# Five small moves in a hybrid decoder trunk: a transfer, two warming matmuls, a maximum, gated products and transposes

## The chip, the cores and the metric

The kernel runs on one core of one Trainium2 chip. The metric is the device time of one execution in microseconds; the median of three runs stands for a kernel. A trace of one more execution shows every instruction of the five engines: TensorE (PE, its weight loads PEld), VectorE (DVE), ScalarE (ACT), GpSimd (POOL) and SyncE (SP, which only issues DMAs).

## The reference

Two layers of a decoder trunk on x of 256 tokens by 2048 features, float32. Cut to what matters here:

```python
# layer 0: h = rms_norm(x); u, v, q, f, i, g = split(h @ w_in)   (1024 columns each)
u = gelu(u); v = rms_norm(gelu(v) per head)
mixed = einsum('hts,bcshd->bcthd', tril(sp_w), v) + sp_b          # gMLP, chunks of 128 tokens
y_a = u * mixed
lb = cumsum(softmax(hgrn_gamma))[0]                               # the "lower bound", 8 heads x 128
# HGRN2, 8 heads: forget gate f' = lb + (1 - lb) * sigmoid(f), k = (1 - lb) * sigmoid(-f),
# o = linear recurrence over q, k, i with decay f'
y_b = rms_norm(o) * silu(g)
x = x + concat(y_a, y_b) @ w_out
x = x + conv_ffn(rms_norm(x))
# layer 1: forgetting attention, 16 heads: scores + c_t - c_s, where
c = cumsum(log_sigmoid(f + b_f))
# softmax, times v, times sigmoid(g), @ w_out; then conv_ffn again
```

## The kernel before

Activations are kept feature-major. Every product with a weight matrix is made at nearly float32 precision from three fast matmuls: an operand is split into a high part and a remainder, and high by high, high by remainder and remainder by high are summed. So each weight chunk (128 x 1024 float32, 512 KB) is loaded by a DMA on SP's queue into `w` (L196), copied by ACT into `wh` (L207), and DVE subtracts the copy from `w` into `wl` (L212). PE then runs twelve matmuls of 512 columns on the chunk (L268 to L270 in `project_tok`, L288 to L290 in `project_four`). `w` has four buffers, `wh` and `wl` three.

The order is written by hand and by a planner. Ahead of each weight chunk the program calls `tick()`, which advances every waiting generator by one step, up to its next `yield`. Side work (norms, heads, gates, transpositions) is written as such generators: one `yield` more puts what follows one weight chunk later. `after(n, g)` starts a generator n + 1 ticks later, and `LAG` (6) ticks are allowed for a transposition to land. A scheduler then gives each engine a fixed order of instructions, by priority and by times of its own; it may take an independent instruction earlier than it is written. `sum_in`, `act_in`, `copy_in`, `mm_in` and `turn_in` tie an instruction behind the latest weight split (`deep["sub"]`), weight copy (`deep["act"]`) or matmul (`deep["main"]`) written so far, so that it can't be taken earlier. At run time every engine works in order: an instruction that waits holds up all that stands behind it.

The start: x comes in seven tiles (1, 1, 2, 2, 2, 4 and 4 of its 16 row blocks). The first is issued on SP, the second on ACT's queue (L87); then the first chunks of the `w_v` projection follow on SP, in halves of 256 KB for the first four (`single` in `weights`), with the other x tiles between them (`AHEAD`, `BEHIND`). `in_order` keeps that order. `WARM` matmuls of 128 columns on a tile of ones (L169) run before the first weights are there; each is two instructions in the trace.

Layer 0 then runs these projections, eight weight chunks each: v (two), f, q, i, f, q, i, u (two), g (two), then the output in four quarters, of which the first two are interwoven. Around the change:

- `mixer_ab` computes lb (L526 to L549) right after v is written. It begins with a maximum over `gam`, which is a part of `pp` that a DMA on ACT's queue brings in late (`fetch_late`); Exp, a reciprocal and products follow, and five small DMAs on POOL's queue spread the result over the partitions (`od`, `orow`).
- `hgrn(h)` is the work of one recurrence head, spread over the ticks of the following projections: products over levels (L601 to L620), scores on PE and their masked copies and additions into `st` on DVE (L625 to L642), then two empty steps, the transpose of `st` on PE (L646, recorded at L165), and one step later the products with i, the mean square (Ln and Exp on ACT, L346, L347) and the scaled copies (L662). `st` and `s128` have three buffers.
- `spatial(j, z)` (L727) waits until all heads are done, takes the gelu of four row blocks of u, and multiplies each into `mg` (L734, recorded at L159), with the split into high part and remainder (L322, L324) as `yB[b]`, one block per step. The output projection reads `yB[0..7]` first. The transposed u (`turn`, tag `QK`, two buffers) stays until its four products are done; the transposed gates of `gated` use the same two buffers.
- `forget()` in `mixer_c` computes c: a scaled copy `ft` on ACT, two transposes on PE (L809, recorded at L165), log-sigmoid, a scan, a store and row broadcasts by POOL's queue, one step apart.
- ACT's functions come in table sets: `act` (L95) loads a set when the function written next needs another (L98), and instructions of one set stay together.

Of the kernel before, what the change touches and what calls it, by code (L numbers as in the profile page):

```python
# [12 lines left out]
ALU = mybir.AluOpType  # L13
# [15 lines left out]
JOIN = 12  # L29
HALF = 8  # L30
EPS = 1e-6
WARM = 7
AHEAD = {2: 2, 4: 4, 6: 6}
BEHIND = {6: 8, 8: 12}
LANE = 64
# [19 lines left out]
def tile_trunk(ctx: ExitStack, tc: tile.TileContext, x, pp_d, cst_d, mlev_d, msk_d,  # L55
               w_v, w_f, w_g, w_i, w_q, w_u, w_abo, w_cf, w_cqkv, w_cg, w_co, w_up, w_dn, spw_d, spb_d, out):
    nc = tc.nc
    V, SC, PE = nc.vector, nc.scalar, nc.tensor
# [20 lines left out]
    fetch = {c0: (t, x[:, c0:c0 + n, :]) for t, c0, n in xload}  # L79
# [4 lines left out]

    first_dma = nc.sync.dma_start(*fetch[0])
    SC.dma_start(pp[:, 0:C_FFN], pp_d[:, 0:C_FFN])
    SC.dma_start(*fetch[1])  # L87
    V.memset(ones, 1.0)
    V.memset(one1, 1.0)
    ident = cst[:, K_ID:K_ID + P]  # L90
# [24 lines left out]
    def bank(tag="px"):  # L115
        n = nm(tag)
        return px.tile([P, 512], F32, tag=tag, name=n, bufs=banks[tag])
# [34 lines left out]
    def act_in(*args, **kw):  # L152
        return behind(act(*args, **kw), "act")
# [4 lines left out]
    def sum_in(*args):  # L158
        return behind(V.tensor_tensor(*args), "sub")  # L159
# [17 lines left out]
    def in_order(r, key="dma"):  # L177
        if key in deep:
            tc.add_manual_dep(r.ins, deep[key].ins.name, order, reason="queue order")
        deep[key] = r  # L180


    def weights(src, n, rows=None, single=None):
        deep["turn"] += 1
        if deep["pool"] is not None and deep["turn"] > 12 and deep["turn"] % 2:
            pool, nw, ns = deep["pool"], 2, 2
        else:
            pool, nw, ns = wp, 4, 3
        w = pool.tile([P, n], F32, tag="w", name=nm("w"), bufs=nw)
        wh = pool.tile([P, n], F32R, tag="wh", name=nm("wh"), bufs=ns)  # L190
        wl = pool.tile([P, n], F32R, tag="wl", name=nm("wl"), bufs=ns)
        parts = [slice(i, i + n // 2) for i in (0, n // 2)] if single else [slice(0, n)]
        for i, p in enumerate(parts):
            if single and i == 0 and single[1] in AHEAD:
                in_order(nc.sync.dma_start(*fetch[AHEAD[single[1]]]))
            r = nc.sync.dma_start(  # L196
                w[:, p] if rows is None else w.rearrange("p (m c) -> p m c", m=rows), src[:, p] if single else src)
            if single:
                in_order(r)
            deep["dma"] = r  # L200
        for i, p in enumerate(parts):
            if single:
                norm, k = single
                r = norm.feed_split(k + i, SC if k + i else V)
                if k + i:
                    in_order(r, "first")
            deep["act"] = SC.activation(wh[:, p], w[:, p], AF.Copy)  # L207
            if single:
                in_order(deep["act"], "first")
            if deep["turn"] == 5:  # L210
                deep["hold"] = deep["act"]
            deep["sub"] = V.tensor_tensor(wl[:, p], w[:, p], wh[:, p].bitcast(F32), ALU.subtract)  # L212
        return wh, wl
# [206 lines left out]
    def mixer_ab(norm):  # L420
# [107 lines left out]
        mx, sm_, lb, omlb = (gm[:, i * NH:(i + 1) * NH] for i in range(4))  # L528
        ge = gm[:, 4 * NH:7 * NH]
        g3 = [gam[:, i * NH:(i + 1) * NH] for i in range(3)]  # L530
        e3 = [ge[:, i * NH:(i + 1) * NH] for i in range(3)]
        V.tensor_tensor(mx, g3[0], g3[1], ALU.max)
        V.tensor_tensor(mx, mx, g3[2], ALU.max)
        for i in range(3):
            V.tensor_tensor(e3[i], g3[i], mx, ALU.subtract)
# [56 lines left out]
        def hgrn(h):  # L592
            l, t = lf[h], kq[h]
            d0 = (h % 4) * P
            SC.activation(l, l, AF.Identity, bias=lb[:, h:h + 1], scale=omlb[:, h:h + 1])
            st = hp.tile([P, 2, P], F32, tag="st", name=nm("st"), bufs=3)
            V.tensor_tensor(st, ident.unsqueeze(1).to_broadcast([P, 2, P]),
                            dgc[:, h].unsqueeze(2).to_broadcast([P, 2, P]), ALU.mult)
            yield

            V.tensor_tensor(t[:, 1::2], t[:, 1::2], view(l, P, (-P, 2), (1, P)), ALU.mult)  # L601
            E = hp.tile([P, NL, 2, P], F32, tag="E", name=nm("E"), bufs=2)
            tot = l
            tots = hp.tile([P, S], F32, tag="tot", name=nm("tot"), bufs=1)
            for li in reversed(range(NL)):
                n = LEVELS[li]
                m = P // n
                for sl in range(2):
                    SC.activation(E[:, li, sl].rearrange("p (b two n) -> p b two n", two=2, n=n),
                                  view(t, 2 * P * sl, (2 * n, 64 // n), (P + n, 2), (1, n)), AF.Copy)  # L610
                if not li:
                    ends = view(t, 0, (P + n, 2), (1, n))
                    V.tensor_tensor(ends, ends, view(tot, 1, (1, 2), (0, n)), ALU.mult)
                    break
                even = view(t, 0, (2 * P, 2), (2 * n, 64 // n), (1, n))
                odd = view(t, P + n, (2 * P, 2), (2 * n, 64 // n), (1, n))
                V.tensor_tensor(even, even, view(tot, 1, (m, 2), (2, m // 2), (0, n)), ALU.mult)
                V.tensor_tensor(odd, odd, view(tot, m, (-m, 2), (2, m // 2), (0, n)), ALU.mult)
                nt = tots[:, S - 2 * m:S - m]
                V.tensor_tensor(nt, view(tot, 0, (2, m)), view(tot, 1, (2, m)), ALU.mult)  # L620
                tot = nt
                if n in (4, 16):
                    yield
            yield
            smk = hp.tile([P, NL * P], F32, tag="smk", name=nm("smk"), bufs=1)  # L625
            for c0, c1 in ((0, 4), (4, NL)):
                sps = bank()
                for li in range(c0, c1):
                    mm_in(sps[:, (li - c0) * P:(li - c0 + 1) * P],
                          E[:, li, 0], E[:, li, 1], start=True, stop=True)  # L630
                if c0 == 0:
                    xps = bank()
                    mm_in(xps[:, 0:P], t[:, 0], t[:, 1], start=True, stop=True)
                    s128 = hp.tile([P, P], F32, tag="s128", name=nm("s128"), bufs=3)
                    SC.activation(s128, xps[:, 0:P], AF.Copy)
                V.tensor_tensor(smk[:, c0 * P:c1 * P], sps[:, 0:(c1 - c0) * P],
                                msk[:, c0 * P:c1 * P], ALU.mult)
                for li in range(c0, c1):
                    n = LEVELS[li]
                    sv = view(st[:, 1], 0, (2 * n, 64 // n), (n - P, 2), (1, n))  # L640
                    V.tensor_tensor(sv, sv, smk[:, li * P:(li + 1) * P].rearrange(
                        "p (b two n) -> p b two n", two=2, n=n), ALU.add)  # L642
            yield
            yield
            op = bank()
            turn_in(op[:, S:S + P], st[:, 1], ident)  # L646
            SC.activation(st[:, 1], op[:, S:S + P], AF.Copy)
            yield
            while len(itoks) <= h // 4:
                yield  # L650
            itok = itoks[h // 4]
            i0, i1 = (itok[:, T, d0:d0 + P] for T in range(2))
            mm_in(op[:, 0:P], st[:, 0], i0, start=True, stop=True)
            PE.matmul(op[:, P:S], s128, i0, start=True, stop=False)
            PE.matmul(op[:, P:S], st[:, 1], i1, start=False, stop=True)
            so = hp.tile([P, LANE], F32, tag="so", name=nm("so"), bufs=2)[:, 0:2]
            for T in range(2):
                SC.activation(itok[:, T, d0:d0 + P], op[:, T * P:(T + 1) * P], AF.Square,
                              accum_out=so[:, T:T + 1])
            rsq(so, so, P)  # L660
            for T in range(2):
                SC.activation(itok[:, T, d0:d0 + P], op[:, T * P:(T + 1) * P], AF.Copy, scale=so[:, T:T + 1])  # L662
            left[0] -= 1
# [63 lines left out]
        def spatial(j, z):  # L727
            while left[0] or j and yB[4 * j - 1] is None:
                yield
            act_in(z, z, AF.Gelu)  # L730
            for i in range(4):
                b = 4 * j + i
                m = mg[b].rearrange("p (t n) -> p t n", t=2)
                sum_in(m, m, natural(z[:, i]), ALU.mult)  # L734
                yB[b] = quad("ya")
                split(yB[b], mg[b], turn=True)
                yield

        for j in range(2):
# [15 lines left out]
    def mixer_c(norm):  # L755
# [44 lines left out]
        def forget():  # L800
# [2 lines left out]
            V.memset(on, 1.0)  # L803
            for T in range(2):
                SC.activation(ft[:, T, 0:CH], pa[T][:, 0:CH], AF.Copy, scale=Rt[:, T:T + 1])
            yield
            ps = bank()
            for T in range(2):
# [405 lines left out]
```

## Time and profile before

| | us |
|---|---|
| median of 3 runs | 2293.24 |
| lowest, highest | 2291.91, 2293.32 |
| the profiled execution | 2294.66 |
| its span, first to last instruction | 2292.5 |
| PE busy | 2284.6 |
| DVE busy | 1561.7 |
| ACT busy | 1314.6 |
| POOL busy | 420.3 |

Matmuls are pipelined: the next one starts 0.23 us after a 512-column matmul, while the trace models an end 0.39 us after the start. So busy time of PE hides short losses, and the distance between two starts shows them. In rows of the timeline the columns are start (us from the span's start), length of the merged group (us), engine, line, operation, tile written and tiles read, count, and in brackets the idle time before and what ended it. "q" behind an engine means its queue, which issues or waits. The list of waits has who waited, for whom, us in total, times and the longest. The profiled execution's granted TensorE clock is given as 1.000; the half speed at the very start shows in the spacing of matmuls alone.

### The profile page before, as it was taken

How to read it: one execution, taken by the hardware profiler on the slowest of the kernel's cores; microseconds unless marked ns; L12 is line 12 of the kernel's file. 1: busy time of each engine (PE TensorE's matmuls, PEld its weight loads, DVE VectorE, ACT ScalarE, POOL GpSimd, SP SyncE). 2: the span in 40 equal slices, each digit the busy share in tenths (PEclk: the TensorE clock that was granted, in tenths of full speed). 3: DMA queues.
4: the chain of work that ended last, by engine and by line, in shares of the span. 5: the costliest groups of instructions: out<-in, count | busy, mean ns of one | idle time of the engine just before them, and what ended most of it. 6: DMA issues, size and time to landing. Idle time of an engine off the chain costs nothing.

```text
span 2292.5 us, 31357 instructions
## 1 busy us (share of the span) xinstructions
PE 2284.6 (100%) x10370; PEld 1899.8 (83%) x10370; DVE 1561.7 (68%) x2374; ACT 1314.6 (57%) x1955; POOL 420.3 (18%) x779
## 2 busy tenths in 40 slices
PE   9999999999999999999999999999999999999999
PEld 7888888888888888888888888888888888888887
DVE  6888767776557656765866665767776467657766
ACT  7677656665456545653555556656665455455643
POOL 0211323212012002111322212232211022012102
PEclk9999999999999999999999999999999999999999
DMA  8655677777667666776676656777777667667765
GB/s 277 213 176 174 188 222 222 239 226 214 202 196 228 212 198 211 221 216 185 176 234 212 198 177 187 214 224 235 232 218 216 195 208 218 211 205 215 220 205 175
DMA packets 487188, 481.05 MB, mean 210 GB/s; under 512 B 102801, under 2 KB 454177, under 8 KB 487025
## 3 DMA queue, kind: packets, MB, share of 16 engines
q1 hardware_dynamic: 459360, 448.29, 63.0%
q0 software_dynamic: 25360, 27.37, 4.9%
q10 hardware_dynamic: 2304, 3.39, 0.4%
q8 instruction: 81, 1.33, 0.2%
q14 instruction: 83, 0.67, 0.1%
HBM read 434.85 MB, written 2.12 MB: 191 GB/s over the span
## 4 chain that ended last, share of the span: by engine, by line
PE 96%; DVE 1%; ACT 1%; DMA 1%; issue 0%; POOL 0%; SPq 0%; DVEq 0%; ACTq 0%
PE pm L290 27%; PE pm L289 27%; PE pm L288 27%; PE pm L269 4%; PE pm L268 4%; PE pm L270 4%; PE px L162 1%; PE pm L259 1%; DVE wl L212 0%; ACT wh L207 0%; DMA w<-in_w_cqkv 0%; DMA pp<-in_pp 0%; PE px L165 0%; PE pm L233 0%; ACT L98 0%
## 5 line engine op out<-in xcount | busy, mean ns | idle before, releaser
L212 DVE TENSOR_TENSOR wl<-w,wh 128x1024 fp32r<-128x1024 f32 (+1 forms) x812 | 986.2, 1217 | 634.1 <-ACT wh L207 630.4
L207 ACT ACTIVATE wh<-w 128x1024 fp32r<-128x1024 f32 (+1 forms) x812 | 854.4, 1054 | 770.9 <-PE pm L290 580.0
L288 PE MATMUL pm<-wh,a 128*128 128x512 f32 x1792 | 700.0, 391 | 0.0
L289 PE MATMUL pm<-wl,a 128*128 128x512 f32 x1792 | 697.6, 389 | 1.0 <-DVE wl L212 1.0
L290 PE MATMUL pm<-wh,a 128*128 128x512 f32 x1792 | 697.5, 389 | 0.0
L314 POOL DMA_DIRECT2D zt<-tmp x413 | 223.6, 549 | 1199.4 <-DVE tmp L308 983.1
L289 PEld LDWEIGHTS pm<-wl,a 128*128 128x128 f32 x1792 | 336.6, 188 | 70.9 <-DVE wl L212 1.8
L290 PEld LDWEIGHTS pm<-wh,a 128*128 128x128 f32 x1792 | 336.4, 188 | 70.2
L288 PEld LDWEIGHTS pm<-wh,a 128*128 128x128 f32 x1792 | 336.5, 188 | 69.2
L314 POOL DMA_DIRECT2D turn<-tmp x336 | 182.0, 550 | 557.0 <-DVE tmp L308 315.7
L288 PE MATMUL pm<-wh,hid 128*128 128x512 f32 x688 | 267.6, 389 | 0.0
L289 PE MATMUL pm<-wl,hid 128*128 128x512 f32 x688 | 267.6, 389 | 0.0
L290 PE MATMUL pm<-wh,hid 128*128 128x512 f32 x688 | 267.6, 389 | 0.0
L268 PE MATMUL pm<-wh,a 128*128 128x512 f32 x464 | 183.7, 397 | 0.0
L269 PE MATMUL pm<-wl,a 128*128 128x512 f32 x464 | 181.1, 390 | 0.9 <-DVE wl L212 0.9
L270 PE MATMUL pm<-wh,a 128*128 128x512 f32 x464 | 180.9, 390 | 0.0
L289 PEld LDWEIGHTS pm<-wl,hid 128*128 128x128 f32 x688 | 129.1, 188 | 27.0
L288 PEld LDWEIGHTS pm<-wh,hid 128*128 128x128 f32 x688 | 129.1, 188 | 26.8
L290 PEld LDWEIGHTS pm<-wh,hid 128*128 128x128 f32 x688 | 129.1, 188 | 26.7
L308 DVE STREAM_TRANSPOSE tmp<-z 128x512 f32<-128x512 f32 x132 | 92.3, 706 | 21.1 <-ACT z L993 18.4
L156 ACT ACTIVATE conv<-zt,pp 128x256 f32<-128x256 f32 x176 | 95.3, 588 | 16.0 <-DMA zt<-tmp 11.0
L269 PEld LDWEIGHTS pm<-wl,a 128*128 128x128 f32 x464 | 87.2, 188 | 19.6 <-DVE wl L212 2.4
(220 smaller groups left out, 1928.7 us busy)
## 6 DMA issues: line engine op xcount, KB each, us to landing
w<-in_w_up SPq DMA_DIRECT2D x352, 512.0 KB, 4.4
w<-in_w_dn SPq DMA_DIRECT2D x176, 512.0 KB, 4.5
w<-in_w_cqkv SPq DMA_DIRECT2D x88, 512.0 KB, 4.3
w<-in_w_abo SPq DMA_DIRECT2D x32, 512.0 KB, 4.3
w<-in_w_cg SPq DMA_DIRECT2D x32, 512.0 KB, 4.2
w<-in_w_co SPq DMA_DIRECT2D x32, 512.0 KB, 4.6
zt<-tmp SPq DMA_DIRECT2D x414, 32.0 KB, 2.6
zt<-tmp POOLq DMA_DIRECT2D x413, 32.0 KB, 2.6
```

Source lines behind the costliest of these rows:

```text
L156: return behind(SC.activation(*args, **kw), "act")
L162: return behind(PE.matmul(*args, **kw), "main")
L207: deep["act"] = SC.activation(wh[:, p], w[:, p], AF.Copy)
L212: deep["sub"] = V.tensor_tensor(wl[:, p], w[:, p], wh[:, p].bitcast(F32), ALU.subtract)
L268: PE.matmul(ps[T], ah, h, start=k + i == 0, stop=False)
L269: PE.matmul(ps[T], ah, l, start=False, stop=False)
L270: deep["main"] = PE.matmul(ps[T], al, h, start=False, stop=k + i == KT - 1)
L288: PE.matmul(ps[T], ah, h, start=k + i == 0, stop=False)
L289: PE.matmul(ps[T], ah, l, start=False, stop=False)
L290: deep["mm"] = deep["main"] = PE.matmul(ps[T], al, h, start=False, stop=k + i == n - 1)
L308: V.transpose(tmp.rearrange("p (b m i t) -> p b m i t", b=4, m=4, t=2)[:, :, :, :, T], src(T).rearrange("p (m b j) -> p b m j", m=4, b=4))
L314: qs[(a + b) % len(qs)].dma_start(dst[BLK * b:BLK * (b + 1), :, a * n:(a + 1) * n], tmp[BLK * a:BLK * (a + 1), b * 4 * n:(b + 1) * 4 * n] ...
```

## The change

The second x tile is issued on SP between the two halves of the first weight chunk, and no longer on ACT's queue. Nine warming matmuls run in place of seven. The first maximum of the lower bound is tied behind the last weight split written before it, which is that of the last chunk of the second v projection. In `hgrn` and in `forget` the transposes come one step later. In `spatial` there is a step before the gelu, one after it, and two steps, not one, from one product to the next.

```diff
-WARM = 7
+WARM = 9
...
     first_dma = nc.sync.dma_start(*fetch[0])
     SC.dma_start(pp[:, 0:C_FFN], pp_d[:, 0:C_FFN])
-    SC.dma_start(*fetch[1])
...
         for i, p in enumerate(parts):
+            if single and i and single[1] == 0:
+                in_order(nc.sync.dma_start(*fetch[1]))
             if single and i == 0 and single[1] in AHEAD:
                 in_order(nc.sync.dma_start(*fetch[AHEAD[single[1]]]))
...
-        V.tensor_tensor(mx, g3[0], g3[1], ALU.max)
+        sum_in(mx, g3[0], g3[1], ALU.max)
...  in hgrn, behind the additions into st:
             yield
             yield
+            yield
             op = bank()
             turn_in(op[:, S:S + P], st[:, 1], ident)
...
         def spatial(j, z):
             while left[0] or j and yB[4 * j - 1] is None:
                 yield
+            yield
             act_in(z, z, AF.Gelu)
+            yield
             for i in range(4):
...
                 split(yB[b], mg[b], turn=True)
+                yield
                 yield
...  in forget:
                 SC.activation(ft[:, T, 0:CH], pa[T][:, 0:CH], AF.Copy, scale=Rt[:, T:T + 1])
+            yield
             yield
             ps = bank()
```

## The prediction

> **What bounds the kernel now.** I read the page first, then the list of PE's waits, then the timeline around each wait.
>
> ```profile
> span 2292.5 us, 31357 instructions
> PE 2284.6 (100%) x10370; PEld 1899.8 (83%) x10370; DVE 1561.7 (68%) x2374; ACT 1314.6 (57%) x1955; POOL 420.3 (18%) x779
> ```
>
> TensorE is the bound: 2284.6 of 2292.5 us. No edit removes a matmul of the model, so the change can win only time in which PE stands or runs slowly. Where it stands, the list of waits says (us in total, times, longest):
>
> ```profile
> PE warm L169 <- DVE one L89: 1.1, 1, 1.1
> PE pm L289 <- DVE wl L212: 1.0, 1, 1.0
> PE pm L269 <- DVE wl L212: 0.9, 2, 0.7
> PE pm L259 <- ACT wh L207: 0.8, 1, 0.8
> PE px L165 <- ACT ft L805: 0.4, 1, 0.4
> PE px L165 <- DVE st L641: 0.3, 1, 0.3
> ```
>
> All but the first are touched: L259 by the nine warming matmuls and the x tile, L269 by the lower bound, L289 by the gMLP products, the two L165 by the transposes. These rows understate the loss, since a matmul's modelled end hides a late successor; I take start-to-start spacing instead, 0.23 us for a 512-column matmul at full speed. The profiled execution took 2294.66 us, 2.16 around its span; the median of the runs is 2293.24, 1.42 less. I work out a difference in the trace and take it off the median.
>
> **The start.** Two extra warming matmuls and the second x tile belong together.
>
> ```profile
> 1.05 3.35 PE L169 MATMUL warm<-ones 128*128 128x128 f32 x14 [1.05 <-DVE one L89]
> ...
> 1.18 0.90 SPq L196 DMA_DIRECT2D w<-in_w_v  x2
> ...
> 5.25 2.07 PE L259 MATMUL pm<-wh,a 128*128 128x512 f32 x4 [0.84 <-ACT wh L207]
> ...
> 5.50 0.61 ACT L207 ACTIVATE wh<-w 128x512 fp32r<-128x512 f32 x1
> ...
> 7.12 1.05 PE L259 MATMUL pm<-wl,a 128*128 128x512 f32 x2
> ...
> 9.65 0.63 PE L259 MATMUL pm<-wl,a 128*128 128x512 f32 x2
> ...
> 12.39 0.62 PE L259 MATMUL pm<-wl,a 128*128 128x512 f32 x2
> ...
> 14.94 1.06 ACT L207 ACTIVATE wh<-w 128x1024 fp32r<-128x1024 f32 x1 [0.45 <-DMA w<-in_w_v]
> ...
> 16.04 1.22 DVE L212 TENSOR_TENSOR wl<-w,wh 128x1024 fp32r<-128x1024 f32 x1 [1.02 <-ACT wh L207]
> ...
> 18.74 0.39 PE L269 MATMUL pm<-wl,a 128*128 128x512 f32 x1
> 18.84 1.22 DVE L212 TENSOR_TENSOR wl<-w,wh 128x1024 fp32r<-128x1024 f32 x1
> ...
> 21.46 0.39 PE L269 MATMUL pm<-wl,a 128*128 128x512 f32 x1
> ```
>
> A k takes four matmuls with wh and two with wl. From 7.12 to 9.65 lie six, 0.42 us each; from 9.65 to 12.39 twelve, 0.23 each. So PE runs at half speed until about 9.6, 4.4 us after the unbroken run began at 5.25, although the warming had run from 1.05 to 4.40 before the 0.84 us hole. The seven warming matmuls are 14 instructions in 3.35 us, 0.21 to 0.24 each; four more take 0.85 to 0.96 and end at 5.25 to 5.36. They fill the hole and cost at most 0.11. If what counts is an unbroken run, it now starts at 1.05, and the same 4.4 us put full speed at 5.5 and not 9.6: ten matmuls that took 4.40 us (5.25 to 9.65) take between 2.3 and 2.5, a gain of up to 2.1.
>
> [...]
>
> The feed caps this. The first full weight chunk has its wl ready at 17.26 (16.04 + 1.22) and is first multiplied with it at 18.74: slack 1.48. The next is ready at 20.06 and used at 21.46: slack 1.40. The first one's ACT copy waited for its DMA, so the transfers do not come earlier for a faster PE. **I take 1.40**; ends 0 (the clock opens when it did) and 1.48.
>
> The x tile leaves ACT's queue and is issued on SP between the two halves, so every SP issue behind it comes one issue (0.45 us, half of 0.90) later: the second half, then the chunk and x loads. The first half no longer shares the engines with x, so it may come up to 0.4 sooner (128 KB less of the some 0.5 MB then under way; estimate). The second half's copy at 5.50 shows no wait and would be done by 6.6 if 0.45 late; its first matmul is the seventh, not before 6.8 at mixed speed. Nothing more than 0.5 either way, and both lie under the cap: 0.
>
> **The lower bound.**
>
> ```profile
> 30.86 0.17 DVE L532 TENSOR_TENSOR gm<-pp 128x8 f32<-128x8 f32 x1 [3.76 <-DMA pp<-in_pp]
> ...
> 31.89 0.39 PE L268 MATMUL pm<-wh,a 128*128 128x512 f32 x1
> 32.99 0.50 PE L269 MATMUL pm<-wl,a 128*128 128x512 f32 x1 [0.72 <-DVE wl L212]
> ...
> 38.59 0.50 PE L269 MATMUL pm<-wl,a 128*128 128x512 f32 x1
> 38.93 0.39 PE L270 MATMUL pm<-wh,a 128*128 128x512 f32 x1
> ```
>
> DVE stood 3.76 us at a maximum of eight columns for a transfer, with the next weight split queued behind it. PE lost 1.10 - 0.23 = 0.87, then 0.11 on the matmul after each late one (38.59 to 38.93 is 0.34), twice: **1.09**. Tied behind the last split of the second v projection, the maximum comes long after that transfer, and DVE does not stand. What waits for it (Exp, reciprocal, five small DMAs on POOL's queue) is held behind v's gelu at the end of that stage in any case, since the table order puts Exp there. Ends 0.87 and 1.09.
>
> **The transposes.** Two places, hgrn and forget.
>
> ```profile
> 148.00:175.00 27.00, 26.69 (x139) 22.38 (x138) 23.90 (x75) 23.78 (x57) 6.50 (x12) 1.00 0.57 165
> ...
> 153.23 0.39 PE L288 MATMUL pm<-wh,a 128*128 128x512 f32 x1
> 153.93 0.33 PE L165 MATMUL px<-cst,st 128*128 128x128 f32 x1 [0.31 <-DVE st L641]
> ...
> 180.87 0.39 PE L268 MATMUL pm<-wh,a 128*128 128x512 f32 x1
> 181.42 0.50 PE L269 MATMUL pm<-wl,a 128*128 128x512 f32 x1 [0.17 <-DVE wl L212]
> 181.76 0.40 PE L270 MATMUL pm<-wh,a 128*128 128x512 f32 x1
> 182.26 0.33 PE L165 MATMUL px<-cst,st 128*128 128x128 f32 x1
> ...
> 1149.91 0.28 PE L779 MATMUL pm<-wh,a 128*128 128x256 f32 x1
> 1150.55 0.28 PE L165 MATMUL px<-cst,ft 128*16 128x128 f32 x1 [0.36 <-ACT ft L805]
> ```
>
> In hgrn PE loses 0.47 (153.23 to 153.93) and 0.27 (181.76 to 182.26) at transposes, and 0.32 + 0.11 at the split between them; together 1.17. One step later (a weight chunk, twelve matmuls, 2.7 us and more) the additions into st are done. But the windows row (columns us, PE, PEld, DVE, ACT, POOL) shows DVE busy 23.90 and ACT 23.78 of 27 us: they are nearly the bound in this stage, and PE freed at 153 can run into a late split at 181. In favour: by counting yields, head 0's normalisation (table of Ln and Exp) now falls behind the second sigmoid of the keys instead of ahead of it, and head 2's between two later gates. That makes five table loads where there were seven, one of the two within 139 to 182 us, at 1283 ns:
>
> ```profile
> L98 ACT ACT_TABLE_LOAD x21 | 26.9, 1283 | 2.0 <-PEq L1203 1.7
> ```
>
> **I take 0.75**, ends -0.8 (one more split late) and 1.17. In forget the transposes stood 0.64 - 0.12 = **0.52**; a step later ft is long there. Its DMAs (POOL's queue: the store of c and four row broadcasts) come one step later too; the first scores stand five steps behind the first broadcast by the count of yields, so that costs nothing; without that cover one transfer, some 3 us.
>
> **The gMLP products.**
>
> ```profile
> 258.92 1.43 DVE L159 TENSOR_TENSOR mg<-mg,turn 128x256 f32<-128x256 f32 x4 [2.33 <-ACT turn L102]
> ...
> 260.27 1.43 DVE L324 TENSOR_TENSOR ya<-mg,ya 128x256 fp32r<-128x256 f32 x4
> ...
> 261.24 0.61 PE L288 MATMUL pm<-wh,a 128*128 128x512 f32 x2
> 262.89 0.50 PE L289 MATMUL pm<-wl,a 128*128 128x512 f32 x1 [1.03 <-DVE wl L212]
> ...
> 276.00:298.00 22.00, 22.00 (x99) 18.23 (x98) 15.79 (x24) 12.72 (x16) 6.49 (x12) 1.00 0.70 211
> ```
>
> DVE stands 2.33 us for the gelu and then does four products and three remainders before the split PE needs. PE loses 1.65 - 0.45 = 1.20, and 0.11 after it: **1.31**, ends 0.9 and 1.31. With a step before and after the gelu and every second step for a product, two DVE operations (0.7 us) lie between splits. The second group's last product moves from the second chunk of the second g projection to the second chunk of the output, and the output reads it two chunks later (5.4 us). Gelu and silu now alternate, two more table loads (2.6 us) on ACT, which has 9 of 22 us free there. The turned u tiles leave their buffer later, so the 16 DMAs of the first gate's transposition (12 on POOL, 4 on SP, with weight loads queued behind) wait about a step longer; their readers come five steps later. Cost 0; without that cover 2.7.
>
> **Sum.** 1.40 + 1.09 + 0.75 + 0.52 + 1.31 = 5.07 us. 2293.24 - 5.07 = **2288.2** (profiled execution about 2289.6). All terms at their best give 5.6, so 2287.7; the runs of before lie 1.4 us apart, and for that spread the low end goes 0.9 further, to 2286.8.
>
> **The rivals.** *Half of it comes back*: the stage at 122 to 199 us is bound by DVE and ACT, and what PE gains it gives back at the next split. For it, the windows row; against it, the fewer table loads. It takes 1.2 to 1.5 off: about 2289.5.
>
> *The clock opens when it did*: then the start gives at most 0.2, 2293.24 - 3.87 = 2289.4. For it: the trace holds only one opening; against it, the hole is the only thing that sets the first run apart from the second.
>
> *The change doesn't do what it says*: the planner puts maximum, products or transposes beside the next late operation; half of the three middle terms goes with some of the start: about 2291.5.
>
> *Slower*: a head's closing step (two squares, an inverse root, two scaled copies) now falls into the step of the next head's scores, with two masked copies and seven additions on DVE. If the weight split stands behind both, PE waits at each head. To be slower by 0.2% it must lose 4.6 us beyond the 4.3 that the other terms win, 1.1 per head over eight heads; at 1.5 per head the time is 2293.2 - 4.3 + 12 = 2300.9. Against it: no work is added, the windows row leaves DVE 3.1 and ACT 3.2 us free, and PE's waits of before there come to 1.2 us over all eight heads.
>
> **How the numbers follow.** About 0.2%, 4.6 us, is what a measurement of this kernel tells from no change; the line is 2288.65, close under the forecast. Forecast 0.66 (own range 2286.8 to 2289.2), half back 0.14, clock unmoved 0.09, not as said 0.06, slower 0.05. Of the forecast's 0.66, 0.58 lie below the line, and 0.02 of the rest: faster 0.60, same 0.35, slower 0.05. The range, 2286.8 to 2291.3, takes in the forecast and the first two rivals.
>
> **What would show it.** Right: no hole between warming and the first matmul, 0.23 us spacing from 5.5 to 6.5 us on, the 0.72 wait replaced by one of up to 0.7 near 16 to 20 us (the feed's cap); no DVE wait at L532; no PE wait at L165; products two at a time and no wait near 262; still about 21 table loads. Wrong: half speed until 9 us, a new PE wait over 0.5 us between 140 and 200 us, or one in the output's first four chunks.

## The result: 3.5 us faster, where 5.1 were forecast

| | median, us | lowest, highest | runs |
|---|---|---|---|
| before | 2293.38 | 2291.91, 2295.54 | 22 |
| changed | 2289.84 | 2289.18, 2291.02 | 22 |

The ratio is 0.9984, with a 95 % interval of 0.9979 to 0.9990. The medians lie 3.5 us apart (interval 3.1 to 4.0, from resampled runs). That is a sure gain, but smaller than the 4.6 us of the forecast's line: it is the outcome to which the prediction gave 0.35 ("same"), not the one with 0.60 ("faster"), and it lies inside the range. The profiled execution went from 2294.66 to 2290.4 us. The page of the changed kernel:

```profile
span 2288.6 us, 31373 instructions
PE 2283.1 (100%) x10374; PEld 1899.6 (83%) x10374; DVE 1562.3 (68%) x2374; ACT 1312.1 (57%) x1955; POOL 421.3 (18%) x779
```

The four extra PE instructions are the two warming matmuls. The span lost 3.9 us. PE's waits in the changed kernel (who waited for whom, us in total, times, longest; the line numbers stand up to one off those of before):

```profile
PE warm L168 <- DVE one L88: 1.1, 1, 1.1
PE pm L260 <- ACT wh L208: 0.7, 2, 0.4
PE pm L270 <- DVE wl L213: 0.3, 1, 0.3
PE pm L290 <- DVE wl L213: 0.2, 1, 0.2
```

Both waits of the transposes are gone, and so is the 1.0 near 262 us, which stood in a projection of g: the 0.2 at L290 is another place, near 1585 us. But PE still waits 0.7 at the first chunks, where 0.8 stood, though no longer ahead of its first matmul: now it waits for the second half and for the chunk behind it. The start is where the gain is missing. The changed kernel's timeline there (start, length, engine, line, operation, tiles; in brackets the idle time before and what ended it):

```profile
1.06 4.21 PE L168 MATMUL warm<-ones 128*128 128x128 f32 x18 [1.06 <-DVE one L88]
...
3.93 0.63 ACT L208 ACTIVATE wh<-w 128x512 fp32r<-128x512 f32 x1 [1.46 <-DMA w<-in_w_v]
...
4.92 1.67 PE L260 MATMUL pm<-wh,a 128*128 128x512 f32 x4
...
6.43 0.62 PE L260 MATMUL pm<-wl,a 128*128 128x512 f32 x2
6.67 0.63 ACT L208 ACTIVATE wh<-w 128x512 fp32r<-128x512 f32 x1 [1.71 <-DMA w<-in_w_v]
...
7.35 1.20 PE L260 MATMUL pm<-wh,a 128*128 128x512 f32 x4 [0.30 <-ACT wh L208]
...
9.37 1.19 PE L260 MATMUL pm<-wh,a 128*128 128x512 f32 x4 [0.36 <-ACT wh L208]
...
17.32 1.22 DVE L213 TENSOR_TENSOR wl<-w,wh 128x1024 fp32r<-128x1024 f32 x1 [1.04 <-ACT wh L208]
...
18.59 0.50 PE L270 MATMUL pm<-wl,a 128*128 128x512 f32 x1 [0.31 <-DVE wl L213]
20.11 1.22 DVE L213 TENSOR_TENSOR wl<-w,wh 128x1024 fp32r<-128x1024 f32 x1
21.45 0.44 PE L270 MATMUL pm<-wl,a 128*128 128x512 f32 x1
```

The hole after the warming is gone, and the matmuls are at full speed from 6.0 us on: 0.43 us from the start at 5.49 to the next, 0.28 from the one at 5.92, 0.23 from 6.20 on. But the second half's copy, at 5.50 before, is at 6.67 and now waits for its transfer. The first full chunk has its wl ready at 18.54 (17.32 + 1.22), 1.28 later than before, and is used at 18.59, where before it was 18.74. The second chunk is used at 21.45, before 21.46. PE runs faster and comes to the same place at the same time.

### The profile page after: what moved, and what is told of

It is laid out like the page before. It is cut to its first block, busy times and chain, and to the rows that moved or that the text cites. A ratio compares the mean times of both kernels' runs of the same rounds, so it can differ in the third digit from the quotient of the medians.

```text
span 2288.6 us, 31373 instructions
## 1 busy us (share of the span) xinstructions
PE 2283.1 (100%) x10374; PEld 1899.6 (83%) x10374; DVE 1562.3 (68%) x2374; ACT 1312.1 (57%) x1955; POOL 421.3 (18%) x779
## 3 DMA queue, kind: packets, MB, share of 16 engines
q10 hardware_dynamic: 2160, 3.26, 0.5%
## 4 chain that ended last, share of the span: by engine, by line
PE 98%; DMA 1%; DVE 0%; POOL 0%; ACT 0%; issue 0%; SPq 0%; DVEq 0%; ACTq 0%
PE pm L290 27%; PE pm L291 27%; PE pm L289 27%; PE pm L270 5%; PE pm L271 5%; PE pm L269 5%; PE px L161 1%; DMA w<-in_w_v 1%; PE px L783 1%; PE pm L784 0%; DMA turn<-tmp 0%; PE px L164 0%; PE pm L234 0%; POOL turn L315 0%; DVE wl L213 0%; PE px L878 0%
## 5 line engine op out<-in xcount | busy, mean ns | idle before, releaser
L289 PE MATMUL pm<-wh,a 128*128 128x512 f32 x1792 | 699.9, 391 | 0.0
L290 PE MATMUL pm<-wl,a 128*128 128x512 f32 x1792 | 697.4, 389 | 0.2 <-DVE wl L213 0.2
L290 PEld LDWEIGHTS pm<-wl,a 128*128 128x128 f32 x1792 | 336.5, 188 | 69.9 <-DVE wl L213 0.6
L289 PEld LDWEIGHTS pm<-wh,a 128*128 128x128 f32 x1792 | 336.4, 188 | 69.4
L289 PE MATMUL pm<-wh,hid 128*128 128x512 f32 x688 | 267.6, 389 | 0.0
L290 PE MATMUL pm<-wl,hid 128*128 128x512 f32 x688 | 267.6, 389 | 0.0
L290 PEld LDWEIGHTS pm<-wl,hid 128*128 128x128 f32 x688 | 129.1, 188 | 26.9
L289 PEld LDWEIGHTS pm<-wh,hid 128*128 128x128 f32 x688 | 129.1, 188 | 26.8
```

Source lines behind the costliest of these rows:

```text
L289: PE.matmul(ps[T], ah, h, start=k + i == 0, stop=False)
L290: PE.matmul(ps[T], ah, l, start=False, stop=False)
```

## Experiments

Each kernel ran 11 times beside 33 runs of the kernel before on the same chip. Differences are of medians, with 95 % intervals from resampled runs; negative is faster. The four kernels of a lot shared a chip and can be compared with each other too. From lot to lot the median of the kernel before itself moves (2293.38 to 2294.37 with the first comparison), so kernels of different lots are compared by their differences from it.

| kernel | median | before | difference [95 %] | ratio [95 %] |
|---|---|---|---|---|
| before + x tile | 2294.45 | 2294.16 | +0.3 [-0.4, 1.0] | 1.0001 [0.9992, 1.0010] |
| before + nine warmings | 2292.96 | 2294.16 | -1.2 [-1.8, -0.3] | 0.9996 [0.9987, 1.0005] |
| changed, x tile back | 2289.71 | 2294.16 | -4.5 [-5.4, -3.9] | 0.9981 [0.9973, 0.9990] |
| changed, seven warmings | 2290.87 | 2294.16 | -3.3 [-3.7, -2.4] | 0.9988 [0.9980, 0.9997] |
| before + lower bound tied | 2294.53 | 2293.84 | +0.7 [0.0, 1.2] | 1.0003 [0.9995, 1.0012] |
| before + hgrn's step | 2291.40 | 2293.84 | -2.4 [-2.9, -1.3] | 0.9991 [0.9982, 0.9999] |
| before + gMLP steps | 2292.62 | 2293.84 | -1.2 [-2.4, -0.9] | 0.9995 [0.9986, 1.0004] |
| changed, x back, eleven warmings | 2289.55 | 2293.84 | -4.3 [-5.0, -4.1] | 0.9982 [0.9973, 0.9990] |
| changed, again | 2290.38 | 2294.37 | -4.0 [-5.0, -3.4] | 0.9983 [0.9974, 0.9991] |
| changed, x back, again | 2289.39 | 2294.37 | -5.0 [-5.8, -4.2] | 0.9978 [0.9969, 0.9987] |
| changed, x back, not tied | 2289.47 | 2294.37 | -4.9 [-5.7, -4.3] | 0.9979 [0.9970, 0.9988] |
| before + forget's step | 2294.31 | 2294.37 | -0.1 [-1.1, 0.5] | 0.9998 [0.9989, 1.0007] |

The six single edits sum to -3.9, near the -3.5 and -4.0 of the whole. The agreement is loose: each interval is 1.2 to 1.6 us wide, and two edits, the x tile and the warming, don't simply add, as is shown below.

**The x tile alone** (first lot, with the next three).

```diff
-    SC.dma_start(*fetch[1])
...
+            if single and i and single[1] == 0:
+                in_order(nc.sync.dma_start(*fetch[1]))
```

> The kernel before with the x tile moved alone. Transfer theory: the tile on SP's queue makes the whole feed late, so the first full chunk's wl is ready near 18.5 us (before 17.26) and the second half's copy starts near 6.6 us (before 5.50); the clock opens near 9.6 us as before, the slack of 1.48 us takes it up, and the time is 2293.4, within 0.4 of before. Chance theory: the late feed of the changed kernel belongs to its one profiled execution, wl is ready near 17.3 us here, and the time is the same as before or 0.3 less.

Measured: no gain, +0.3. In its trace the first full chunk's wl is ready at 18.80, in the same band as the changed kernel's 18.54, and the second half's copy starts at 6.37, both as the transfer theory had it.

**The warming alone.**

```diff
-WARM = 7
+WARM = 9
```

> The kernel before with nine warming matmuls alone. Transfer theory: the feed is as before (wl of the first full chunk ready near 17.3 us), PE runs at full speed from 6 us on and meets it, so 1.2 to 1.5 us are won: about 2292.0. Chance theory: the same. If the clock opens near 9.6 us in spite of the warming, nothing is won.

Measured: -1.2; the feed stays early (17.97). So the warming gains by itself.

**The x tile back on ACT's queue**, all else as changed.

```diff
+    SC.dma_start(*fetch[1])
...
-            if single and i and single[1] == 0:
-                in_order(nc.sync.dma_start(*fetch[1]))
```

> The changed kernel with the x tile back on ScalarE's queue. Transfer theory: wl of the first full chunk ready near 17.3 us, 1.2 to 1.4 us less than the changed kernel: about 2288.5. Chance theory: within 0.4 us of the changed kernel's 2289.8.

Measured: -4.5 against before. Its wl is ready at 17.41, and the gain is 1.0 larger than the 3.5 of the changed kernel's first comparison (another chip). Yet in its profiled execution PE came to full speed as late as before, at 9.8 us, with nine warmings.

**Seven warmings in the changed kernel.**

```diff
-WARM = 9
+WARM = 7
```

> The changed kernel with seven warming matmuls. Transfer theory: the late feed hides the slow clock, so the two more warming matmuls win nothing beside the moved tile: 2289.8, within 0.4. Chance theory (the feed is as before in most executions): 1.2 to 1.4 us more, about 2291.1.

Measured: -3.3, against -3.5 and -4.0 for the changed kernel: with the x tile on SP the two more warmings are worth 0.2 to 0.7, which the intervals can't tell from nothing. On the same chip this kernel is 1.2 us slower than the one before it [0.8, 2.4].

**The lower bound alone** (second lot, with the next three).

```diff
-        V.tensor_tensor(mx, g3[0], g3[1], ALU.max)
+        sum_in(mx, g3[0], g3[1], ALU.max)
```

> The kernel before with the lower bound's maximum tied alone. Theory of the prediction: VectorE's 3.76 us wait for the parameters is typical and PE loses 1.09 us by it, so this is 1.1 us less than before. Rival: the wait depends on when that transfer lands; the two kernels that kept the untied order waited 1.1 and 1.3 us and PE lost next to nothing, so this is 0 to 0.4 us less than before, with no VectorE wait in its trace all the same.

Measured: +0.7 [0.0, 1.2], no gain. In its trace DVE does not stand at the maximum, as the edit wants.

**hgrn's step alone.**

```diff
             yield
             yield
+            yield
             op = bank()
```

> The kernel before with the transposes of the recurrence heads one step later alone. Theory: the transposes waited for the additions and two ScalarE table loads go; 1.4 us less than before, five table loads between 100 and 180 us and none of PE's waits at the transposes. Rival of the prediction (half comes back): 0.4 us less or nothing, with a PE wait at a weight split between 140 and 200 us.

Measured: -2.4, the largest single gain. PE's waits in its trace:

```profile
PE pm L259 <- ACT wh L207: 1.3, 1, 1.3
PE warm L169 <- DVE one L89: 1.1, 1, 1.1
PE pm L289 <- DVE wl L212: 1.0, 2, 0.5
PE px L165 <- ACT ft L806: 0.7, 1, 0.7
```

No transpose of hgrn waits for st any more; forget's still waits for ft, and the g projection near 263 us for wl (one of the two at L289, 0.46), since those edits are not in this kernel.

**The gMLP steps alone.**

```diff
+            yield
             act_in(z, z, AF.Gelu)
+            yield
...
                 split(yB[b], mg[b], turn=True)
+                yield
                 yield
```

> The kernel before with the gMLP products spread alone. Theory: the 1.0 us wait of PE near 262 us goes, 1.2 to 1.3 us less than before. Rival: the wait moves to another split of the two g projections or of the output's first chunks, and less than 0.5 us is won.

Measured: -1.2, as forecast. Its table loads are 23, two more than before, and hgrn's step alone has 19; the whole has 21:

```profile
L98 ACT ACT_TABLE_LOAD x23 | 29.5, 1283 | 2.1 <-PEq L1206 1.7
```

**Eleven warmings, x tile back.**

```diff
-WARM = 9
+WARM = 11
```

> The changed kernel with the x tile back on ScalarE's queue and eleven warming matmuls. Transfer theory: the first weights are there near 5.1 us and the first matmul was at 5.8 in both traces with the tile on that queue and nine warming matmuls, a hole of 0.5 us; eleven end at 5.9 and leave no hole, so the clock is open in nearly every execution: 0.3 to 0.8 us less than with nine (4.45 us less than before there), about 4.9 less than before. Rival: the hole of 0.5 us does not matter, and this is the same as with nine or 0.2 us slower, since PE starts 0.1 us later.

Measured: -4.3, no more than with nine (-4.5, -5.0), as the rival had it: the hole of 0.5 us is not worth closing, as far as these runs can tell.

**The changed kernel again, and the x tile back again, side by side** (third lot, with the next two).

> The changed kernel once more, on the same chip as the next. It was 3.5 us less than before in its first comparison: 3.0 to 4.0 less here, with wl of the first full chunk ready near 18.5 us again if the tile on SP's queue makes the feed late, near 17.3 if the first trace was a chance.

> The changed kernel with the x tile back on ScalarE's queue, on the same chip as the changed kernel. Transfer theory: wl of the first full chunk ready at 17.2 to 18.0 us, and 0.7 to 1.2 us less than the changed kernel. Chance theory: the two agree within 0.4 us.

Measured: on one chip the kernel with the x tile back is 1.0 us faster than the changed one [0.1, 1.7]. It beats both kernels, and in its profiled execution the whole list of PE's waits is one row:

```profile
PE warm L169 <- DVE one L89: 1.1, 1, 1.1
```

**The maximum untied, x tile back.**

```diff
-        sum_in(mx, g3[0], g3[1], ALU.max)
+        V.tensor_tensor(mx, g3[0], g3[1], ALU.max)
```

> The changed kernel with the x tile back on ScalarE's queue and the lower bound's maximum untied. If the tie is worth nothing in most executions (the five other traces with the untied order lost no more than 0.2 us there, and the tie alone was 0.0 to 1.2 us slower), this agrees with the run before it within 0.4 us. Theory of the prediction: about 1.1 us slower than it.

Measured: +0.1 [-0.7, 0.9] against the tied one on the same chip. The tie is worth nothing that these runs can tell.

**forget's step alone.**

```diff
                 SC.activation(ft[:, T, 0:CH], pa[T][:, 0:CH], AF.Copy, scale=Rt[:, T:T + 1])
+            yield
             yield
```

> The kernel before with the transposes of the forget gates one step later alone. Theory: PE's wait for ft, 0.5 to 0.8 us of spacing in the five traces that have it, goes: 0.5 to 0.7 us less than before. Rival: the chain behind it is late for the first scores and a wait appears between 1155 and 1200 us, so nothing is won.

Measured: -0.1 [-1.1, 0.5]. The interval holds both nothing and the 0.52.

## Why the prediction was right and wrong, point by point

**The start: 1.40 forecast, about nothing got.** The step that failed is "Nothing more than 0.5 either way, and both lie under the cap: 0." The 1.40 was the slack of the first full chunks, and the move of the x tile used it up. Between 4 and 6 us the windows (us, PE, PEld, DVE, ACT, POOL, clock, share of the DMA engines, GB/s) read, before, changed, and with the tile back (the run beside the repeated changed kernel):

```profile
4.00:6.00 2.00, 1.16 (x4) 0.77 (x4) 1.08 (x3) 1.43 (x3) 0.00 (x0) 1.00 1.04 363
```

```profile
4.00:6.00 2.00, 2.00 (x9) 1.81 (x9) 1.15 (x3) 0.96 (x2) 0.00 (x0) 1.00 0.76 199
```

```profile
4.00:6.00 2.00, 1.85 (x7) 1.47 (x7) 1.27 (x3) 1.27 (x3) 0.00 (x0) 1.00 1.01 361
```

With the tile on SP 179 to 221 GB/s move in these two microseconds (four traces), with it on ACT's queue 325 to 371 (ten traces). The prediction priced the place on SP as one issue, 0.45 us, and took the rate as given. The first half did come earlier, its copy at 3.93 to 4.25 (4.57 to 5.10 with the tile on ACT's queue); I had said up to 0.4. But everything behind it came late. The first full chunk's split on DVE in the third lot, changed kernel, then tile back:

```profile
17.50 1.23 DVE L213 TENSOR_TENSOR wl<-w,wh 128x1024 fp32r<-128x1024 f32 x1 [1.03 <-ACT wh L208]
```

```profile
15.99 1.23 DVE L212 TENSOR_TENSOR wl<-w,wh 128x1024 fp32r<-128x1024 f32 x1 [1.03 <-ACT wh L207]
```

Over all fourteen traces that wl is ready between 18.45 and 18.80 with the tile on SP (four) and between 16.90 and 17.97 with it on ACT's queue (ten): no overlap. The 100th of PE's product matmuls (those with weights) shows that this feed, and not the clock, then sets the pace. With the tile on SP it starts at 29.8 to 30.2 us in all four traces, though PE came to full speed anywhere from 5.3 to 9.6. With the tile on ACT's queue it starts at 28.5 to 29.3 in the six traces with full speed by 6.8 us, and at 29.5 to 30.5 in the four with a later one. So the warming gains only with the tile on ACT's queue (1.2 by itself), and beside it the move of the tile costs 1.0: 0.2 is left of the 1.40. Against the 0.45 us of one issue the first full chunk came 1.3 later in the changed kernel than before (18.54 and 17.26). That the feed then caps the start is shown, by the traces and by the 1.0 us between the two kernels of the third lot. Why the rate falls is open: another place of the tile on SP, or another queue, was not tried. The pages of the two profiles show only that the tile changed its queue with its issuer: q10 has 2304 packets before and 2160 in the changed kernel, the difference being on q1.

The other half of this step, that a gapless run opens the clock early, held in the changed kernel but is too simple a rule. Not the spacing alone shows the opening: the record of a granted clock of 1.0 begins at 9.60 us in the trace of before and at 6.01 in the changed kernel's, and full-speed spacing begins within 0.2 us of it (9.65 and 6.20). For the other kernels I go by the spacing. With nine warmings the last half-speed matmul starts at 5.9 at the latest in four of six traces, at 6.5 in one, and at 9.8 in one, the first run with the x tile back. Its rows, warming and first chunk, where four matmuls at half speed take 2.07 and at full speed 1.2:

```profile
1.05 4.21 PE L169 MATMUL warm<-ones 128*128 128x128 f32 x18 [1.05 <-DVE one L89]
5.78 2.07 PE L259 MATMUL pm<-wh,a 128*128 128x512 f32 x4 [0.52 <-ACT wh L207]
```

With seven warmings it starts at 6.6 or later, up to 10.2, in five of seven. In the other two (the gMLP steps and forget's step alone) the first four matmuls already took full-speed time (1.21 and 1.20 us), in spite of a hole of over one microsecond (1.29 and 1.06); here the former:

```profile
1.06 3.36 PE L169 MATMUL warm<-ones 128*128 128x128 f32 x14 [1.06 <-DVE one L89]
...
5.71 1.21 PE L259 MATMUL pm<-wh,a 128*128 128x512 f32 x4 [1.29 <-ACT wh L207]
```

So neither does a gapless run have to come first, nor does a longer warming make sure of it; at most it raises the odds, and thirteen executions are few to say by how much. A short hole close ahead did not keep the clock shut either, in the changed kernel with seven warmings:

```profile
1.05 3.36 PE L168 MATMUL warm<-ones 128*128 128x128 f32 x14 [1.05 <-DVE one L88]
4.69 2.07 PE L260 MATMUL pm<-wh,a 128*128 128x512 f32 x4 [0.27 <-ACT wh L208]
6.56 0.69 PE L260 MATMUL pm<-wl,a 128*128 128x512 f32 x2
```

The two matmuls at 6.56 take 0.69, where half speed takes 1.05 and full speed 0.62, so the clock opened by 6.9 us; PE had stood 0.27 us up to 4.69, 2.2 us earlier. What sets the moment no run here shows.

**The lower bound: 1.09 forecast, nothing got.** The failed step is the size: "DVE stood 3.76 us" was one landing of one transfer. The wait is in the other five untied traces of before's order too, but shorter. DVE at the maximum with nine warmings alone, hgrn's step alone, the gMLP steps alone:

```profile
27.90 0.17 DVE L532 TENSOR_TENSOR gm<-pp 128x8 f32<-128x8 f32 x1 [1.29 <-DMA pp<-in_pp]
```

```profile
29.68 0.17 DVE L532 TENSOR_TENSOR gm<-pp 128x8 f32<-128x8 f32 x1 [1.90 <-DMA pp<-in_pp]
```

```profile
26.95 0.17 DVE L532 TENSOR_TENSOR gm<-pp 128x8 f32<-128x8 f32 x1 [1.17 <-DMA pp<-in_pp]
```

At 1.1 to 1.9 us the splits catch up and PE loses nothing: from its 50th to its 134th matmul of the model it takes 19.04 to 19.24 us in those five and 19.04 to 19.27 in the tied ones; only the profiled execution of before took 20.19. That execution was 1.42 us above the median of the runs, as the prediction itself says; it then took the whole 1.09 off the median, where five like traces don't have the loss.

**The heads: 0.75 forecast, more got.** Alone the step gave 2.4 [1.3, 2.9]. The mechanism was right: the windows row of 148 to 175 us has PE without a gap, at the same load of DVE (23.74; before 23.90) and less of ACT (22.73; before 23.78).

```profile
148.00:175.00 27.00, 27.00 (x143) 23.03 (x142) 23.74 (x83) 22.73 (x60) 4.67 (x9) 1.00 0.57 170
```

The term was mis-sized. From the 500th to the 1100th product matmul (125 to 286 us before: the heads' stage and nearly all of the g projections) PE takes 160.0 to 160.7 us in the five traces with neither edit, 158.07 with hgrn's step alone (2.0 less than the lowest), 159.13 with the gMLP steps alone (0.9 less) and 157.3 in all seven traces that have both: 2.7 at least, where the two terms came to 0.75 + 1.31 = 2.06. In the trace the two edits add up, and the start's and the maximum's changes do not touch them.

The spacing of these matmuls shows where the 2.0 of hgrn's step come from. The whole 1.17 that the prediction had counted is gone, and nothing of it came back, so the 0.42 held back for that was too much. The rest was not on its list. First, the transpose of a later head waits too, between 225 and 228 us. It cost PE 0 to 0.64 us in the six traces without the step, but only 0.08 in the one that the prediction was read from; with the step it is gone in all eight. With nine warmings alone it reads:

```profile
226.73 0.30 PE L165 MATMUL px<-cst,st 128*128 128x128 f32 x1 [0.48 <-ACT E L609]
```

Second, the wait near 262 us, which stands in the term of the gMLP products, is halved by hgrn's step already, from 1.20 to 0.62 of spacing:

```profile
263.11 0.50 PE L289 MATMUL pm<-wl,a 128*128 128x512 f32 x1 [0.46 <-DVE wl L212]
```

Third, transposes now stand directly beside a head's scores, here in the changed kernel:

```profile
228.02 0.27 PE L164 MATMUL px<-cst,st 128*128 128x128 f32 x1
228.13 1.05 PE L161 MATMUL px<-E 128*128 128x128 f32 x8
```

So small matmuls break the stream of 512-column matmuls 18 times in this stretch and not 21, and each break costs about 0.08 us beside the small matmuls' own time (the first 512-column matmul behind them is followed after 0.31 us, where the stream has 0.23, in both traces), together 0.25.

**The gMLP products: 1.31 forecast, 1.2 got.** The gelu still makes DVE wait as long (2.34; before 2.33), but one product of 0.43, and not four products with three remainders, follows before the split (the list of signs had products two at a time):

```profile
258.52 0.43 DVE L158 TENSOR_TENSOR mg<-mg,turn 128x256 f32<-128x256 f32 x1 [2.34 <-ACT turn L101]
...
259.47 1.23 DVE L213 TENSOR_TENSOR wl<-w,wh 128x1024 fp32r<-128x1024 f32 x1 [0.52 <-ACT wh L208]
...
260.95 0.42 DVE L158 TENSOR_TENSOR mg<-mg,turn 128x256 f32<-128x256 f32 x1
261.28 1.22 DVE L213 TENSOR_TENSOR wl<-w,wh 128x1024 fp32r<-128x1024 f32 x1
```

The table loads are the counted ones, two fewer in hgrn and two more here. The work put at nothing (the 16 DMAs, the later yB) made no wait: PE has none over 0.1 us between 43 and 1130 us.

**forget: 0.52 forecast, 0.1 got, which can't be told from nothing.** In the changed kernel's trace PE's wait is gone:

```profile
1148.36 0.40 PE L271 MATMUL pm<-wh,a 128*128 128x512 f32 x1
1148.59 0.38 PE L164 MATMUL px<-cst,ft 128*16 128x128 f32 x2
1148.73 0.47 PE L269 MATMUL pm<-wh,a 128*128 128x512 f32 x1
1149.04 0.39 PE L270 MATMUL pm<-wl,a 128*128 128x512 f32 x1
```

Alone the edit could not be told from nothing. In its trace two other waits stand in the place of the one for ft: 0.5 at another transpose, for the root of a mean square, and 0.4 to 0.5 at a projection's matmul, the chunk of which came late; PE's waits from 1140 to 1165 us there, and that chunk's copy:

```profile
PE px L165 <- DVE rt L349: 0.5, 1, 0.5
PE pm L269 <- DVE wl L212: 0.4, 1, 0.4
```

```profile
1154.56 1.06 ACT L207 ACTIVATE wh<-w 128x1024 fp32r<-128x1024 f32 x1 [3.74 <-DMA w<-in_w_cqkv]
```

In this stretch all six traces without the edit have the ft wait (0.4 to 0.7) and no other; of the eight with it five have none in the list and three the late chunk. From its 4800th to its 6000th product matmul PE takes 302.3 to 303.1 us in the six (mean 302.7), 301.8 to 302.1 in the five and 302.7 to 303.3 in the three (mean of the eight 302.4). So the edit gains about 0.7 where the chunk is in time, and over all traces about 0.35. Nothing here says that the edit makes the chunk late: counted from the 4800th matmul, ACT starts that copy 28.2 to 31.4 us later without the edit and 28.5 to 30.9 with it. In two traces without the edit the copy came at 31.0 and 31.4, and PE did not wait there; with it PE comes sooner and waits where the copy comes at 30.7 or later. The term took the next chunk to be in time always, and in some executions it is not.

**The rivals.** "Half of it comes back" (2289.5) and "the clock opens when it did" (2289.4) lie nearest to the time, but neither happened: the heads gave nothing back, and the clock was open by about 6.0 us in the profiled execution, and the matmuls at full speed by 5.4 in the second one. "The change doesn't do what it says" fails as well: no other late operation stands in the place of those moved between 43 and 1130 us. The slower rival had no sign: no wait between 140 and 200 us.

**What would show it.** As listed: no hole after the warming, full speed from 6.0 us, a feed wait at 18.59 (0.31), no DVE wait at the maximum, no PE wait at a transpose, products apart, 21 table loads. None of the signs of "wrong" appeared, not even for the start: full speed early was taken as its proof, and the landing of the next chunks, which decided it, was not on the list.

**In sum**, by the runs: start 0.2 for 1.40 (1.0 more is had by leaving the x tile where it was), lower bound nothing for 1.09 (-0.7 [-1.2, 0.0] alone, 0.1 [-0.7, 0.9] with the x tile back; minus is a loss), heads 2.4 for 0.75, forget 0.1 for 0.52, products 1.2 for 1.31. Three terms too high were in part made good by one too low. The total came near by luck, because errors cancelled.

## What to carry to other kernels

Before a wait is priced from one trace, ask whether what it waits for varies: a transfer that lands late in one execution is worth its average over executions, and a profile shows one draw (DVE stood 3.76 us at the maximum in the one trace, 1.1 to 1.9 in the other five). A gain capped by the feed is only as good as the claim that the feed stays put, so an edit that moves an early transfer has to be costed together with the one that uses the slack. A small wait that comes back in every execution, as the transposes' did, is worth more than a large one that one trace happens to show.

## What the runs showed of the hardware

- Moving one 128 KB load from ACT's queue to SP, between two halves of a weight chunk, lowered the rate between 4 and 6 us from 325-371 GB/s (ten traces) to 179-221 (four), and the first full chunk was ready at 18.45 to 18.80 us, not 16.90 to 17.97.
- The time at which PE comes to full speed varies from run to run of like kernels: with seven warmings from 5.5 or before to 10.2 us, with nine from 5.3 to 9.8. In the one trace with eleven it is 5.3.
- The 512-column matmul that starts first behind small ones is followed later: from 1148.73 to 1149.04 lie 0.31 us, where the stream has 0.23.
- Transfers late in the kernel vary too: at the addition that reads the turned output DVE stood 1.90 us in the changed kernel (near 1581 us) and 2.85 with the lower bound alone (near 1586), in the same code, and PE then waited 0.15 and 0.75 us for a split. This may be some of the 1 to 4 us by which runs of one kernel differ.
